# A hybrid attention block on one core: an unused table of taps leaves its buffer to a tile of the compressor's weight

## The chip, the core and the metric

The program runs on one core of a Trainium2 chip. The metric is the device time of one execution in microseconds (us), as the median of several runs. The profile is of one more execution, with its own time. Engines are TensorE (PE; its weight loads are PEld), VectorE (DVE), ScalarE (ACT), GpSimd (POOL) and SyncE (SP, which here only issues loads and stores).

## What is computed

One transformer layer on x of 256 tokens by 1024 features, all in float32: a projection, four mixers side by side (a sparse attention with a compressor, a block attention, a depthwise convolution of 31 taps, a gated recurrence), an output projection, and a feed-forward part of width 4096 between two layer norms.

```python
h = x @ w_in                                   # split by columns into the mixers' inputs
kc = nsa_compress(kc, pe, w1, b1, w2)          # gelu((blocks + pe) @ w1 + b1) @ w2, for k and for v
o_nsa  = nsa_attention(q_n, kc, vc, ks, vs, kw, vw, gates, rel_tab[:4])
o_moba = moba_attention(q_m, k_m, v_m, rel_tab[4:])
o_conv = conformer_conv(conv_in, dw_w, dw_b, cln_g, cln_b, pw_w)
o_hgrn = hgrn2_mixer(q_h, f_h, i_h, g_h, lb, hn_g)
x = layer_norm(ALPHA * x + concat(o_nsa, o_moba, o_conv, o_hgrn) @ w_out, ln1_g, ln1_b)
x = layer_norm(ALPHA * x + square(relu(x @ w_ff1)) @ w_ff2, ln2_g, ln2_b)
```

## The kernel before

**Weights.** Each weight comes in as a raw float32 tile of 128 partitions by 2048 columns, from the pool `raws` (L168), which holds five of them. For most, `Weight.split` (L234) then makes a pair: ACT rounds the raw tile to `hi` (L245), DVE subtracts to get `lo` (L246), and PE multiplies hi by hi, hi by lo and lo by hi. The pools `his` and `los` hold three tiles each. Three chunks (ca, cg, qn) and km are multiplied raw. The projection's weight is cut into chunks by columns, named ca, cg, n1, ni0, ni1, qn, f, q, km, g, qm, vm; "ni0" and "ni1" are two halves of one chunk by rows. In the profile's names the last digits are cut off, so w_n is n1 and w_ni is ni0 or ni1.

**The compressor's weight** w1 comes in four tiles of 1 MB, in two loads of two (`load_w1`, L419: w1a for c = 0, w1b for c = 1). The profile calls them `w<-in_nsa_cmp_w_dram`. `part_cmp` multiplies them in L686, 8 products for each tile, into one bank of PSUM.

**The taps.** L488 and L489 load a table of the convolution's taps, 1 MB, from GpSimd's queue into the tile `tapw`, which has the buffer `mixl` of the pool `wk`. Only the branch `if CONV_T` of `part_conv` would read it, and `CONV_T` is empty. The convolution is done by DVE alone, 62 operations on `yc` (L571, L573). The next tile in that buffer is `mixl`, the low part of the mixers' outputs, written first by the end of the windowed attention.

**Order.** SP issues all loads of weights in the order of the list LOADS as the table below puts them. A load waits for its buffer (the engines that last read it) and for the load that had its semaphore before it: the eight `DMAHW` lanes go round. Each engine works strictly in the order that is written down for it in the table ISSUE (L69), one string of instruction numbers for each engine, so an instruction that waits holds all behind it. The first stage, up to about 112 us, is projections and mixers; then come w_out, the first norm, 16 groups of feed-forward, and the second norm.

**Banks.** The projections' products go to two banks named `mm` (L202), in turn. A chunk's product can begin only when ACT or DVE has copied the bank's content before it: for q and f that is ni's, which ACT copies to `vn` (L645) and `iv` (L345).

Of the kernel before, what the change touches and what calls it, by code (L numbers as in the profile page):

```python
# [9 lines left out]
F32 = mybir.dt.float32  # L10
# [7 lines left out]
P = 128  # L18
S = 256
# [27 lines left out]
def shape_constants():  # L47
# [13 lines left out]
    for i, b in enumerate(LEVELS):  # L61
# [63 lines left out]
    ),  # L125
    Activation=(
# [9 lines left out]
    ),  # L136
    Pool=(
        "20-22 14 23-24 15 2 9-10 13 11-12 0-1 3-8 16-19 25-28 "
    ),
    SP=(  # L140
        "0-10 30 28-29 11-27 31-89 "
# [21 lines left out]
def layer(ctx, tc, I, const, out):  # L163
# [18 lines left out]
    CONV_T = ()  # L182

    LOADS = "ca cg n1 ni0 qn f ni1 qm w1a q km g w1b vm".split()
# [234 lines left out]
    def load_w1(c):  # L419
        res = []  # L420
        at_(R_SPLIT + next(chunk_no))
        for i in range(2):
            raw = raws.tile([P, 2048], F32, name="w1", tag="raw").rearrange("p (a b) -> p a b", a=8)
            nc.sync.dma_start(raw, I["nsa_cmp_w1"][:, c, i])
            res.append(raw)
        return res
# [60 lines left out]

    tapw = wk.tile([P, 8, 8, 32], F32, name="tapw", tag="mixl")  # L488
    late(tapw, I["taps"])  # L489
# [49 lines left out]
    def part_conv():  # L539
        nonlocal pcv, yc  # L540
        at_(K["taps"])
        yc = t2_("c", "yc")
        if CONV_T:

            W, H, n = 28 + S, 31 + S, len(CONV_T)
            hc_d = dr.tile([P, n, H], F32, name="hc_d")
            G.dma_start(hc_d, hc[:, CONV_T[0]:CONV_T[0] + n])
            hcs = wk.tile([P, n, 4, W], F32, name="hcs", tag="hgw")
            for i in range(n):
                for j in range(4):  # L550
                    G.dma_start(hcs[32 * j:32 * j + 32, i],
                                bass.AP(tensor=hc_d.tensor, offset=hc_d.offset + i * H + j,
                                        ap=[[n * H, 32], [32 * n * H, 4], [1, W]]))

            pcv = hbank([P, n, S])
            for i in range(n):
                for b in range(8):
                    for q in range(4):
                        T.matmul(pcv[32 * q:32 * q + 32, i], tapw[:, 4 * CONV_T[i] + q, b], hcs[:, i, q, 4 * b:4 * b + S],
                                 start=(b == 0), stop=(b == 7))  # L560
# [3 lines left out]
        for k in range(31):  # L564
            for i in range(2):
                if i in CONV_T:
                    continue
# [649 lines left out]
```

## Time and profile before

| | us |
|---|---|
| median of 3 runs | 332.45 (331.56 to 332.95) |
| the profiled execution, its own time | 335.78 |
| its span, first to last instruction | 334.0 |
| PE busy in the span | 319.8 (96%) |
| DVE busy | 233.3 (70%) |
| ACT busy | 166.8 (50%) |
| POOL busy | 10.5 (3%) |
| DMA moved | 62.75 MB, mean 188 GB/s |

Busy is the time in which an engine had an instruction running; for PE the ends of products are modelled. "Waits" are idle time of an engine ahead of an instruction, put down to the event that came last. The timeline gives instructions in order of time, equal neighbours merged. Times in it are from the span's start; the profiled execution took 3.33 us more than the median of the runs.

### The profile page before, as it was taken

What the parts mean: (1) busy time and instruction counts of PE and PEld (TensorE: products, weight loads), DVE (VectorE), ACT (ScalarE), POOL (GpSimd) and SP (SyncE); (2) the same over time, 40 slices, a digit from 0 to 9 for tenths busy, and PEclk for the clock granted to TensorE, in tenths of its full rate; (3) what the DMA queues carried; (4) which work ended last, traced back from release to release, by engine and by line L of the source; (5) the groups of instructions that cost most, each with busy time, mean ns of one, the idle gap of its engine ahead of it and who ended that gap; (6) DMA issues with size and microseconds to landing.
All of it is one profiled execution on the core that took longest, in us unless ns stands there. A gap on an engine that the chain in (4) does not pass through costs nothing.

```text
span 334.0 us, 4992 instructions
## 1 busy us (share of the span) xinstructions
PE 319.8 (96%) x1929; PEld 273.1 (82%) x1929; DVE 233.3 (70%) x428; ACT 166.8 (50%) x307; POOL 10.5 (3%) x33
## 2 busy tenths in 40 slices
PE   8999969999999999989999999999999999999990
PEld 6897859898988778788888888888888888888880
DVE  0269969999989866886677477747564756568286
ACT  1464444784899982344365354535453545373100
POOL 3500000000000100000000000100000000000000
PEclk9999998999999999999999999999999999999996
DMA  7999799094300216556567555965565646520012
GB/s 234 387 398 416 235 395 388 15 371 135 121 0 2 54 74 251 153 226 186 214 232 251 176 203 155 318 202 207 153 226 160 219 144 233 156 98 0 2 49 77
DMA packets 18359, 62.75 MB, mean 188 GB/s; under 512 B 1784, under 2 KB 3664, under 8 KB 17696
## 3 DMA queue, kind: packets, MB, share of 16 engines
q1 hardware_dynamic: 15648, 56.61, 47.8%
q0 software_dynamic: 1056, 3.72, 3.2%
q10 hardware_dynamic: 1632, 2.11, 2.2%
q8 instruction: 15, 0.25, 0.3%
q14 instruction: 8, 0.07, 0.1%
HBM read 61.37 MB, written 1.06 MB: 187 GB/s over the span
## 4 chain that ended last, share of the span: by engine, by line
PE 86%; DVE 8%; DMA 2%; ACT 1%; issue 1%; DVEq 0%; ACTq 0%
PE mm L1102 15%; PE mm L1100 8%; PE hg L1121 5%; PE hg L1122 4%; PE tt L1122 4%; PE tt L1120 4%; PE hg L1120 4%; PE tt L1121 4%; DMA w_q_raw<-in_w_in_dram 2%; PE mm_km L310 2%; PE mm L1099 2%; PE mm_cg L310 2%; DVE yc L573 2%; PE acc L292 1%; PE tt L371 1%; PE tt L397 1%
## 5 line engine op out<-in xcount | busy, mean ns | idle before, releaser
L1102 PE MATMUL mm<-x1s,w_hi 128*128 128x512 f32 x210 | 74.4, 394 | 0.0
L246 DVE TENSOR_TENSOR r_lo<-r_raw,r_hi 128x1024 fp32r<-128x1024 f32 x40 | 47.4, 1221 | 24.8 <-ACT r_hi L245 24.8
L1100 PE MATMUL mm<-x1s,w_lo 128*128 128x256 f32 x240 | 61.0, 279 | 0.0
L245 ACT ACTIVATE r_hi<-r_raw 128x1024 fp32r<-128x1024 f32 x40 | 40.6, 1050 | 33.5 <-PE tt L1122 32.4
L1100 PEld LDWEIGHTS mm<-x1s,w_lo 128*128 128x128 f32 x240 | 44.9, 188 | 2.7
L1102 PEld LDWEIGHTS mm<-x1s,w_hi 128*128 128x128 f32 x210 | 39.2, 188 | 7.4
L246 DVE TENSOR_TENSOR w_lo<-w_raw,w_hi 128x1024 fp32r<-128x1024 f32 x32 | 37.8, 1218 | 5.0 <-ACT w_hi L245 5.0
L245 ACT ACTIVATE w_hi<-w_raw 128x1024 fp32r<-128x1024 f32 x32 | 32.2, 1051 | 4.6 <-DMA w_raw<-in_w_ff_dram 4.5
L1106 ACT ACTIVATE fx<-mm 128x256 f32<-128x256 f32 x30 | 11.4, 383 | 44.4 <-PE mm L1102 44.4
L1107 DVE TENSOR_TENSOR fs<-mm,fx 128x256 f32<-128x256 f32 x30 | 12.6, 424 | 28.5 <-ACT fx L1106 28.5
L573 DVE SCALAR_TENSOR_TENSOR yc<-hc,cols,yc 128x256 f32<-128x256 f32 x60 | 27.5, 479 | 0.5
L1121 PE MATMUL hg<-r_lo,fh 128*128 128x512 f32 (+1 forms) x70 | 26.4, 378 | 0.0
L1120 PE MATMUL hg<-r_hi,fh 128*128 128x512 f32 (+1 forms) x70 | 26.4, 377 | 0.0
L1121 PE MATMUL tt<-r_lo,fh 128*128 128x512 f32 x64 | 24.1, 396 | 0.0
L1122 PE MATMUL hg<-r_hi,fl 128*128 128x512 f32 (+1 forms) x70 | 22.4, 376 | 0.0
L1122 PE MATMUL tt<-r_hi,fl 128*128 128x512 f32 x64 | 20.8, 397 | 0.0
L1120 PE MATMUL tt<-r_hi,fh 128*128 128x512 f32 x64 | 20.8, 396 | 0.0
L1121 PEld LDWEIGHTS hg<-r_lo,fh 128*128 128x128 f32 x70 | 13.2, 189 | 2.7
L1122 PEld LDWEIGHTS hg<-r_hi,fl 128*128 128x128 f32 x70 | 13.2, 189 | 2.6
L1120 PEld LDWEIGHTS hg<-r_hi,fh 128*128 128x128 f32 x70 | 13.2, 188 | 2.1
L1121 PEld LDWEIGHTS tt<-r_lo,fh 128*128 128x128 f32 x64 | 12.1, 188 | 2.9
L1122 PEld LDWEIGHTS tt<-r_hi,fl 128*128 128x128 f32 x64 | 12.1, 189 | 2.8
(331 smaller groups left out, 650.7 us busy)
## 6 DMA issues: line engine op xcount, KB each, us to landing
w_raw<-in_w_ff_dram SPq DMA_DIRECT2D x32, 512.0 KB, 4.4
r_raw<-in_w_ff_dram SPq DMA_DIRECT2D x16, 1024.0 KB, 4.9
w<-in_nsa_cmp_w_dram SPq DMA_DIRECT2D x4, 1024.0 KB, 7.6
r_raw<-in_w_out_dram SPq DMA_DIRECT2D x4, 1024.0 KB, 6.1
w_ni_raw<-in_w_in_dram SPq DMA_DIRECT2D x2, 792.0 KB, 11.4
xf<-in_xt_dram ACTq DMA_DIRECT2D x4, 256.0 KB, 6.9
w_ca_raw<-in_w_in_dram SPq DMA_DIRECT2D x4, 256.0 KB, 7.1
w_cg_raw<-in_w_in_dram SPq DMA_DIRECT2D x2, 512.0 KB, 5.8
```

The costliest lines, as they stand in the source:

```text
L245: A.activation(self.h[:, i:j], self.raw[:, i:j], AF.Copy)
L246: self.last = V.tensor_tensor(self.l[:, i:j], self.raw[:, i:j], self.h[:, i:j].bitcast(F32), op=ALU.subtract)
L310: T.matmul(dst[:, i], w.raw[:, k, P * i:P * i + P], xf[:, k], start=(k == 0), stop=(k == KT - 1))
L573: V.scalar_tensor_tensor(yc[:, i], h, w, yc[:, i], op0=ALU.mult, op1=ALU.add)
L1099: T.matmul(flat(pf[i]), h, flat(x1s[:, k]), start=True, stop=False)
L1100: T.matmul(pf[i][:, 0], l, x1h[:, k], start=False, stop=False)
L1102: T.matmul(flat(pf[i]), h, flat(x1s[:, k]), start=False, stop=(k == KT - 1))
L1106: A.activation(lo[:, i], pf[i][:, 1], AF.Copy)
L1107: V.tensor_tensor(sq[:, i], pf[i][:, 0], lo[:, i], op=ALU.add)
L1120: T.matmul(bank_, h, w.h[:, i, sl], start=(g == 0 and i == 0), stop=False)
L1121: T.matmul(bank_, h, w.l[:, i, sl], start=False, stop=False)
L1122: last = T.matmul(bank_, l, w.h[:, i, sl], start=False, stop=(g == NG - 1 and i == 1 and sl.stop != 768))
```

## The change

The table of taps, its tile, its load and the branch that would read it go, on the host too. In `load_w1` the first of the four tiles (c = 0, i = 0) takes the buffer `mixl` in place of one of the five raw ones. In LOADS q moves ahead of w1a. The table ISSUE is new: for PE, DVE and ACT in the first stage, for POOL by one number less, and for SP, where one load (the tile in `mixl`) moves ahead of three small ones. No arithmetic changes.

```diff
@@ ISSUE, one line of PE's and the whole of SP's @@
-        "0-10 12 11 13-14 16 18 15 17 19 21 20 23-35 22 40-41 36 42 37-38 43-45 39 46-81 88-91 82-83 92-95 84-87 "
+        "0-6 8 7 10 9 12 11 13-14 16 15 17 19 18 21 23-33 20 34 22 35 40 36-37 41-46 38 47-59 39 60-79 88-91 80-87 "
...
-        "0-10 30 28-29 11-27 31-89 "
+        "0-10 18 30 28-29 11-17 19-27 31-89 "
@@ layer @@
-    CONV_T = ()
-
-    LOADS = "ca cg n1 ni0 qn f ni1 qm w1a q km g w1b vm".split()
+    LOADS = "ca cg n1 ni0 qn f ni1 qm q w1a km g w1b vm".split()
@@ load_w1 @@
-            raw = raws.tile([P, 2048], F32, name="w1", tag="raw").rearrange("p (a b) -> p a b", a=8)
+
+            pool, tag = (raws, "raw") if c or i else (wk, "mixl")
+            raw = pool.tile([P, 2048], F32, name="w1", tag=tag).rearrange("p (a b) -> p a b", a=8)
             nc.sync.dma_start(raw, I["nsa_cmp_w1"][:, c, i])
@@ layer @@
-    tapw = wk.tile([P, 8, 8, 32], F32, name="tapw", tag="mixl")
-    late(tapw, I["taps"])
@@ part_conv @@
-        if CONV_T:
...
-                if i in CONV_T:
-                    continue
```

In the rows of the order, a name's number is the buffer's, `[waits ...]` lists the engines and lanes whose signal the instruction waits for, and lines of the changed kernel are numbered some 3 to 30 lower. The first place is SP's queue from the load of f to that of q. Before:

```order
L228 DMA w_f_raw_126<-in_w_in_dram 128x1024 [waits DMAHW2_49,PE_49]
L228 DMA w_f_raw_126<-in_w_in_dram 128x1024 [waits DMAHW3_49]
L228 DMA w_ni1_raw_135<-in_w_in_dram 128x1584 [waits DMAHW4_49,PE_49]
L228 DMA w_qm_raw_141<-in_w_in_dram 128x1024 [waits DMAHW5_49,DVE_49]
L228 DMA w_qm_raw_141<-in_w_in_dram 128x1024 [waits DMAHW6_49]
L424 DMA w1_150<-in_nsa_cmp_w1_dram 128x2048 [waits DMAHW7_49,DVE_49]
L424 DMA w1_152<-in_nsa_cmp_w1_dram 128x2048 [waits DMAHW0_49,PE_49]
L228 DMA w_q_raw_154<-in_w_in_dram 128x1024 [waits DMAHW4_49,DMAHW2_49,DVE_49]
L228 DMA w_q_raw_154<-in_w_in_dram 128x1024 [waits DMAHW3_49]
```

and now, from the tile in `mixl` on:

```order
L423 DMA w1_159<-in_nsa_cmp_w1_dram 128x2048 [waits DMAHW7_49]
L904 DMA pw_1269<-in_conv_pw_w_dram 128x2x256 [waits DMAHW0_49]
L664 DMA w2_685<-in_nsa_cmp_w2_dram 128x128 [waits DMAHW1_49]
L666 DMA w2k_687<-in_nsa_cmp_w2_dram 128x256 [waits DMAHW2_49]
L225 DMA w_f_raw_126<-in_w_in_dram 128x1024 [waits DMAHW3_49,DVE_49]
L225 DMA w_f_raw_126<-in_w_in_dram 128x1024 [waits DMAHW4_49]
L225 DMA w_ni1_raw_135<-in_w_in_dram 128x1584 [waits DMAHW5_49,PE_49]
L225 DMA w_qm_raw_141<-in_w_in_dram 128x1024 [waits DMAHW6_49,PE_49]
L225 DMA w_qm_raw_141<-in_w_in_dram 128x1024 [waits DMAHW7_49]
L225 DMA w_q_raw_150<-in_w_in_dram 128x1024 [waits DMAHW0_49,DVE_49]
L225 DMA w_q_raw_150<-in_w_in_dram 128x1024 [waits DMAHW1_49]
L423 DMA w1_161<-in_nsa_cmp_w1_dram 128x2048 [waits DMAHW3_49,PE_49]
```

The load of q has moved ahead of w1a and waits for other lanes and another DVE operation; one w1a tile (w1_159) stands ahead of f, the other (w1_161) behind q.

The second place is ACT around the copy of q's weight, w_q_hi, and the copies that empty ni's two banks, vn and iv (their ends release the banks for the products mm_q and mm_f). Before:

```order
L245 ACTIVATE w_qm_hi_144<-w_qm_raw_141 128x1024 [waits DMAHW5_49,DVE_49,PE_49]
L245 ACTIVATE w_qm_hi_144<-w_qm_raw_141 128x1024 [waits DMAHW6_49]
L245 ACTIVATE w_q_hi_157<-w_q_raw_154 128x1024 [waits DMAHW2_49,DVE_49,PE_49]
L645 ACTIVATE vn_410<-mm_ni0_360 128x140
L645 ACTIVATE vn_410<-mm_ni0_361 128x140
L194 ACTIVATE gate_416<-vn_410 128x24 [waits Activation_49]
L345 ACTIVATE iv_413<-mm_ni0_361 128x256
L345 ACTIVATE iv_413<-mm_ni0_360 128x256
```

and now:

```order
L242 ACTIVATE w_qm_hi_144<-w_qm_raw_141 128x1024 [waits DMAHW6_49,PE_49]
L619 ACTIVATE vn_408<-mm_ni0_359 128x140 [waits PE_49]
L619 ACTIVATE vn_408<-mm_ni0_358 128x140 [waits PE_49]
L242 ACTIVATE w_q_hi_153<-w_q_raw_150 128x1024 [waits DMAHW0_49,DVE_49]
L191 ACTIVATE gate_414<-vn_408 128x24 [waits Activation_49]
L342 ACTIVATE iv_411<-mm_ni0_359 128x256
L192 ACTIVATE gate_414<-gate_414 128x24 [waits Activation_49]
L342 ACTIVATE iv_411<-mm_ni0_358 128x256
L242 ACTIVATE w_q_hi_153<-w_q_raw_150 128x1024 [waits DMAHW1_49]
```

Both copies to vn have moved ahead of w_q_hi, and the second half of w_qm_hi has gone behind iv.

The third place is PE where the products of q end and those of w1b (w1_175, w1_177) begin. Before:

```order
L315 MATMUL mm_q_422<-xs_87,w_q_lo_158 128x256
L313 MATMUL mm_q_422<-xs_87,w_q_hi_157 128x256
L314 MATMUL mm_q_422<-xs_87,w_q_hi_157 128x256
L315 MATMUL mm_q_422<-xs_87,w_q_lo_158 128x256
L686 MATMUL acc_654<-w1_175,blk0_333 32x256 [waits DMAHW1_49]
L686 MATMUL acc_654<-w1_177,blk1_334 32x256 [waits DMAHW2_49]
```

and now:

```order
L312 MATMUL mm_f_534<-xs_87,w_f_lo_130 128x256
L311 MATMUL mm_q_420<-xs_87,w_q_hi_153 128x256
L312 MATMUL mm_q_420<-xs_87,w_q_lo_154 128x256
L660 MATMUL acc_652<-w1_161,blk1_332 32x256
L660 MATMUL acc_652<-w1_159,blk0_331 32x256
L660 MATMUL acc_652<-w1_161,blk1_332 32x256
L660 MATMUL acc_652<-w1_175,blk0_331 32x256 [waits DMAHW1_49]
L660 MATMUL acc_652<-w1_177,blk1_332 32x256 [waits DMAHW2_49]
L660 MATMUL acc_652<-w1_175,blk0_331 32x256
```

Three products of w1a have moved from ahead of mm_q to this place. On SP the loads that feed it were before:

```order
L228 DMA w_g_raw_166<-in_w_in_dram 128x1024 [waits DMAHW7_49,DVE_49]
L228 DMA w_g_raw_166<-in_w_in_dram 128x1024 [waits DMAHW0_49]
L424 DMA w1_175<-in_nsa_cmp_w1_dram 128x2048 [waits DMAHW1_49,PE_49]
L424 DMA w1_177<-in_nsa_cmp_w1_dram 128x2048 [waits DMAHW2_49,PE_49]
L228 DMA w_vm_raw_179<-in_w_in_dram 128x1024 [waits DMAHW3_49,DVE_49,Activation_49]
```

and are now:

```order
L225 DMA w_g_raw_166<-in_w_in_dram 128x1024 [waits DMAHW7_49,DMAHW4_49,DVE_49]
L225 DMA w_g_raw_166<-in_w_in_dram 128x1024 [waits DMAHW0_49]
L423 DMA w1_175<-in_nsa_cmp_w1_dram 128x2048 [waits DMAHW1_49,DVE_49]
L423 DMA w1_177<-in_nsa_cmp_w1_dram 128x2048 [waits DMAHW2_49,DVE_49]
L225 DMA w_vm_raw_179<-in_w_in_dram 128x1024 [waits DMAHW3_49,PE_49]
```

The two tiles of w1b now wait for DVE in place of PE (their buffers were those of qm and q, which DVE's w_qm_lo and w_q_lo read last), and vm, behind them, for PE.

## Rows read from the trace of the kernel before

**Rows 1.** Waits of PE, whole span: waited for, us in total, times, longest.

```profile
PE mm_q L313 <- ACT iv L345: 2.6, 1, 2.6
...
PE mm_ni L335 <- ACT qn L345: 0.7, 1, 0.7
PE mm_ni L336 <- DVE w_ni_lo L246: 0.2, 1, 0.2
```

**Rows 2.** Windows before and after that wait: PE, PEld, DVE, ACT, POOL busy, clock, DMA share, GB/s.

```profile
33.00:43.40 10.40, 9.68 (x52) 8.79 (x52) 10.28 (x19) 4.02 (x4) 0.00 (x0) 1.00 0.83 252
...
48.39:51.75 3.36, 3.36 (x16) 3.36 (x17) 3.33 (x14) 3.10 (x13) 0.00 (x0) 0.51 1.04 423
```

**Rows 3.** Timeline of ACT, 46 to 48.6 us: start, us, what, [idle before <-releaser].

```profile
46.40 1.06 ACT L245 ACTIVATE w_q_hi<-w_q_raw 128x1024 fp32r<-128x1024 f32 x1 [5.42 <-DMA w_q_raw<-in_w_in_dram]
47.37 0.45 ACT L645 ACTIVATE vn<-mm_ni 128x140 f32<-128x140 f32 x2
47.84 0.22 ACT L194 ACTIVATE gate<-vn 128x24 f32<-128x24 f32 x1
47.97 0.64 ACT L345 ACTIVATE iv<-mm_ni 128x256 f32<-128x256 f32 x2
```

**Rows 4.** Timeline of SP's issues, 22 to 47 us; the time spans a group's issues.

```profile
22.89 3.12 SPq L228 DMA_DIRECT2D w_qm_raw<-in_w_in_dram  x2
28.90 4.31 SPq L424 DMA_DIRECT2D w<-in_nsa_cmp_w_dram  x2
39.10 1.07 SPq L228 DMA_DIRECT2D w_q_raw<-in_w_in_dram  x2
...
46.23 0.87 SPq L424 DMA_DIRECT2D w<-in_nsa_cmp_w_dram  x2
```

**Rows 5.** Waits of SP's queue, whole span.

```profile
SPq L228 <- DVE w_ni_lo L246: 5.8, 1, 5.8
```

**Rows 6.** Timeline of PE, 43 to 66 us.

```profile
43.48 1.93 PE L686 MATMUL acc<-w,blk 128*32 128x256 f32 x32
45.34 0.49 PE L371 MATMUL tt<-ksw,qn 64*128 64x128 f32 x4
48.39 0.57 PE L313 MATMUL mm_q<-xs,w_q_hi 128*128 128x256 f32 x1 [2.55 <-ACT iv L345]
...
63.28 1.93 PE L686 MATMUL acc<-w,blk 128*32 128x256 f32 x32
```

**Rows 7.** Timeline of DVE, 27 to 62 us.

```profile
27.08 1.80 DVE L246 TENSOR_TENSOR w_ni_lo<-w_ni_raw,w_ni_hi 128x1584 fp32r<-128x1584 f32 x1
...
47.49 1.23 DVE L246 TENSOR_TENSOR w_q_lo<-w_q_raw,w_q_hi 128x1024 fp32r<-128x1024 f32 x1 [2.93 <-ACT w_q_hi L245]
...
50.91 1.22 DVE L246 TENSOR_TENSOR w_q_lo<-w_q_raw,w_q_hi 128x1024 fp32r<-128x1024 f32 x1
...
57.65 4.40 DVE L573 SCALAR_TENSOR_TENSOR yc<-hc,cols,yc 128x256 f32<-128x256 f32 x9
```

**Rows 8.** DMA issues: out<-in, queue, count, KB each, median us from issue to landing.

```profile
r_raw<-in_w_ff_dram SPq DMA_DIRECT2D x16, 1024.0 KB, 4.9
w<-in_nsa_cmp_w_dram SPq DMA_DIRECT2D x4, 1024.0 KB, 7.6
r_raw<-in_w_out_dram SPq DMA_DIRECT2D x4, 1024.0 KB, 6.1
...
tapw<-in_taps_dram POOLq DMA_DIRECT2D x1, 1024.0 KB, 11.2
```

**Rows 9.** Windows late in the first stage, columns as in rows 2.

```profile
75.00:90.00 15.00, 15.00 (x121) 13.80 (x122) 14.65 (x47) 9.22 (x24) 0.00 (x0) 1.00 0.41 141
...
100.00:112.00 12.00, 12.00 (x128) 9.84 (x121) 11.00 (x35) 11.64 (x32) 0.00 (x0) 1.00 0.01 2
```

**Rows 10.** Window of the first projections, columns as in rows 2.

```profile
5.60:33.00 27.40, 27.24 (x147) 24.00 (x145) 14.97 (x27) 12.26 (x21) 6.02 (x12) 1.00 1.04 401
```

**Rows 11.** Timeline of ACT near 29 us.

```profile
29.43 0.38 ACT L581 ACTIVATE ksw<-mm_n 128x256 f32<-128x256 f32 x1 [4.29 <-PE mm_n L315]
```

More of the change, by code (lines that the diff above doesn't have):

```diff
@@ L111 @@
     DVE=(
[13 rows of a table removed]
[13 rows of a table added]
     ),
     Activation=(
[9 rows of a table removed]
[9 rows of a table added]
     ),
     Pool=(
-        "20-22 14 23-24 15 2 9-10 13 11-12 0-1 3-8 16-19 25-28 "
+        "19-21 13 22-23 14 2 8-9 12 10-11 0-1 3-7 15-18 24-27 "
     ),
     SP=(
-        "0-10 30 28-29 11-27 31-89 "
+        "0-10 18 30 28-29 11-17 19-27 31-89 "
     ),
@@ L539, in part_conv @@
     def part_conv():
-        nonlocal pcv, yc
+        nonlocal yc
         at_(K["taps"])
         yc = t2_("c", "yc")
-        if CONV_T:
[L545 to L560, printed above, removed]
-            for i, c in enumerate(CONV_T):
-                A.activation(yc[:, c], pcv[:, i], AF.Identity, bias=cols[:, R_DB + c:R_DB + c + 1])
         at_(K["tapv"])
@@ L1181, in lay_out @@
                            for r, i, j in CHUNKS.values()], axis=1)
-    dw = a["conv_dw_w"][0]
-    taps = np.zeros((4, 32, 8, 8, 32), np.float32)
-    for k in range(31):
-        for c in range(32):
-            taps[(k + 1) % 4, c, :, (k + 1) // 4, c] = dw[k, c::32]
     brow = np.zeros((40, P), np.float32)
@@ L1192, in lay_out @@
     ff1 = a["w_ff1"][0].reshape(8, P, 16, 256).transpose(1, 2, 0, 3)
-    out = dict(x=a["x"], xt=tiles(a["x"][0].T), w_in=w_in, cols=rows.T, taps=taps.reshape(P, 8, 8, 32), brow=brow,
+    out = dict(x=a["x"], xt=tiles(a["x"][0].T), w_in=w_in, cols=rows.T, brow=brow,
                nsa_cmp_w1=w1, nsa_cmp_w2=w2, rel_bias=a["rel_bias"].T, w_ff1=ff1)
```

91 rows, old and new, of tables (Activation, DVE, PE) are left out of this document.

## Prediction

> **What bounds the kernel now.** I read PE's waits first. PE is busy for 96% of the span, so what can be gained quickly is where it stands still. In the first stage that is one place: mm_q waits 2.6 us; the two waits of mm_ni add 0.7 and 0.2 [rows 1]. The page puts mm_q's wait down to the copies to iv. ACT's timeline shows what was behind that: ACT stood idle for 5.42 us until q's weight had landed, and only then did w_q_hi, and behind it in strict order vn, gate and iv, which empty the two banks that mm_q and mm_f need [rows 3]. So mm_q had lost its weight and its bank to one late load. SP's timeline shows why it was late: q was issued at 39.10, behind the two w1a tiles (28.90 to 33.21) [rows 4], and its queue had waited 5.8 us for DVE's w_ni_lo to free a raw buffer [rows 5].
>
> The wait costs more than itself. PE came back at 48.39 [rows 6], and until 51.75 the granted clock was 0.51, the 1.2 GHz level of 2.4 [rows 2]. After the 0.7 us wait at mm_ni the clock stayed at 1.00 [rows 2]. The second engine to look at is DVE: 14.65 of 15 us are busy late in the stage, where PE has no wait, and ACT is as full in the last 12 us [rows 9].
>
> **The change part by part.** The durations are of the profiled execution, 335.78 us. That is 3.33 above the median of 332.45, so I take differences from there and set them against the median.
>
> *The table, 1 MB.* Its load leaves POOL's queue, and a w1 tile of the same size takes its place among the loads of that time, so the bytes up to about 30 us stay the same. In that stretch DMA is full, 401 GB/s at a share of 1.04 [rows 10]; the table took 11.2 us to land, where 1 MB of w1 took 7.6 [rows 8]. Nobody read it. Its one descriptor issue on POOL has no one behind it who is waited for. Worth nothing by itself; the branch that goes held no instruction.
>
> *q earlier.* One raw buffer is freed for q, since a w1a tile sits in mixl. q now waits for the first w_ni_lo, which ended at 28.88 (27.08 + 1.80) [rows 7] and stands earlier in the new order, and on SP it is behind qm, issued by 26.0 [rows 4]. So q goes out by 28.9 in place of 39.10 and, at the 7.3 us that it needed (46.40 less 39.10), lands by 36.2. It is then needed at 43.5. The late load is gone with 7 us to spare.
>
> *What is late next at mm_q.* ni's last product ended at 43.48, where w1a's products begin [rows 6]. Four small products have moved out from among ni's (0.49 us by the like row), so it ends at 43.0. From there ACT has vn 0.45, w_q_hi 1.06, gate 0.22, iv 0.64 and a second gate 0.22, together 2.6 us [rows 3]: banks free at 45.6, w_q_hi at 44.5. PE meanwhile has w1a, 1.93, less three of its 16 products, 0.36, and twice 0.49 [rows 6]: it arrives at 43.0 + 2.55 = 45.55. The two meet; the wait falls from 2.55 to about 0.05. **Gain 2.5 us.**
>
> *The clock.* 3.36 us at 0.51 would have been 1.71 at full clock. Without the wait there is nothing before it that the trace shows lowering the clock. **Gain 1.65 us.**
>
> *Small waits.* The new order has mm_ni wait for other copies. At best both old waits go (0.9 us); at worst DVE sets the pace. DVE restarts with w_q_lo at 44.5, 3.0 us before 47.49 [rows 7], but half of w_qm_lo (1.22, as w_q_lo) is still to be done. So it is 1.8 us earlier where PE is 4.2 earlier: 2.4 us could come back. I take 0.35, nearer the good end, because the free filler is large: in DVE's queue nine yc operations stand in a row (4.40 us) [rows 7], which no other engine needs before the convolution's end. **Loss 0.35 us, between -0.9 and 2.4.**
>
> *w1b, loads made later.* Its two tiles were issued at 46.23 [rows 4] and now wait for DVE's w_qm_lo and w_q_lo. From w_q_lo's first half to the end of its second, DVE took 4.64 us (47.49 to 52.13) [rows 7]; the new order puts five yc (0.49 each) and half of w_qm_lo (1.22) between: 8.3 us, so the second tile goes out at 44.5 + 8.3 = 52.8. Landing takes 4.9 to 7.6 us for 1 MB [rows 8]: 57.7 to 60.4. I take 5.5, between the two lower rows, as the queue then holds little else: 58.3. PE needs it at 45.6 + 14.9 (48.39 to 63.28 before [rows 6]), less 1.65 of clock, less four transposes that leave (0.49), plus three w1a products (0.36): 58.7. Covered by 0.4 us; the cover before was some 8. vm goes out behind it, when PE has left w1a, some 6 us later than now; its copies on ACT then come at most 1 or 2 us late, and its products are the stage's filler.
>
> *The rest of the new order, POOL's and the tail.* Same instructions, other places; after the first stage PE has no wait by a load. Nothing.
>
> A rule of the Trainium skill speaks against the move of the tile (DMA: Bandwidth & Descriptors, section on queues, rings and completion order): each DMA engine takes turns between queues that have work, while one queue's descriptors begin in order. By it the table on POOL's queue let SP's loads through by turns, and a tile in SP's own queue lets none through. By the bytes alone f lands when it did; by that rule it could land later by the tile's whole time, rival B below.
>
> Sum: 2.5 + 1.65 - 0.35 = 3.8 us; 335.78 becomes 331.98, the median 332.45 becomes **328.65**.
>
> **The rivals.**
>
> *A. DVE sets the pace.* For it: 14.65 of 15 us busy [rows 9], and DVE gets ahead by less than PE. Against: the filler. The loss is 2.4 in place of 0.35: 330.7 us.
>
> *B. f is late.* w1's tile is ahead of f on SP's queue, and the new order has ACT copy f's weight before ksw, which before waited for PE alone, at 29.43 [rows 11]. 1 MB at 401 GB/s [rows 10] is 2.6 us, and a wait of that length has once brought 1.65 us of low clock: 4.25 against a gain of 4.15 (before the small waits), so 332.55. Against: the bytes ahead of f are the same as with the table.
>
> *C. w1b comes late (the slower side).* One mechanism: SP's queue stands until DVE has done w_q_lo, and PE stands at w1b's first products. At 7.6 us a load, landing at 60.4, PE waits 1.7 and loses 1.65 of clock: 332.0. From a landing at 60.85 the gain of 3.8 is eaten (2.15 + 1.65); from 62.5 the kernel is slower by over 0.5%. That needs DVE 2 us later than worked out, say because a reduction that stands ahead of w_q_lo waits for the bias tile. At 63.3: 4.6 + 1.65 - 3.8, so 334.9.
>
> *D. The wait stays in part.* q is there, but w_q_hi, vn and iv still lie between ni's end and mm_q on ACT; if ACT comes 1.5 us late to them, that and the clock remain: 331.8.
>
> **How the numbers follow.** Forecast 0.60, A 0.13, B 0.10, C 0.12, D 0.05. Low end: 332.45 less 4.15 and both small waits, 327.4. High end: 332.2, which takes in A and D and the mild half of C; B's full price and C's bad half, some 0.16, are left out. A measurement can tell about 0.5% (1.66 us) from no change: faster is below 330.8, slower above 334.1. Faster: the forecast, half of A, a little of D: 0.68. Slower: C's bad half and a part of B: 0.10. The rest, 0.22, is no change.
>
> **What would show it.** Right: q issued before 30 us; no wait at mm_q over 0.3 us; granted clock 1.00 from 46 to 60; PE's w1b products at about 59 and everything after it some 4 us earlier. A wait of PE at w1b's first product speaks for C, DVE idle nowhere and several PE waits on DVE between 60 and 112 for A, ACT's w_f_hi idle on DMA for B. A time above 331 makes the prediction wrong.

## The result and the profile after

The changed kernel takes **334.9 us** (median of 6 runs, 334.03 to 335.86), the kernel before 332.54 (6 runs, 331.56 to 332.95). The ratio is 1.0077 with an interval of 1.0055 to 1.0099: slower by 0.8%, where a gain was forecast, 328.65 in a range of 327.4 to 332.2. Of 91 further executions of before one took 338.86 us, the others 331.44 to 333.69.

The profiled execution is one of the six, 334.85 us with a span of 333.1; in it PE is busy for 320.9 us (96%), DVE for 234.2, ACT for 167.3 and POOL for 10.0, and DMA moved 61.70 MB, the 1 MB of the table less.

Yet the profile after shows the steps that the prediction worked out. These are issues of SP's queue:

```profile
18.75 0.81 SPq L225 DMA_DIRECT2D w_f_raw<-in_w_in_dram  x2
...
21.47 3.56 SPq L225 DMA_DIRECT2D w_qm_raw<-in_w_in_dram  x2
25.51 0.80 SPq L225 DMA_DIRECT2D w_q_raw<-in_w_in_dram  x2
...
49.60 2.28 SPq L423 DMA_DIRECT2D w<-in_nsa_cmp_w_dram  x2
```

q goes out at 25.51 in place of 39.10 [rows 4]. PE's waits have no mm_q left, and none at w1b:

```profile
PE acc L1025 <- DVE scale L1018: 1.5, 1, 1.5
PE acc L289 <- DVE idle L286: 1.2, 1, 1.2
PE mm_ni L332 <- DVE blk L569: 0.6, 1, 0.6
PE hg L1025 <- DVE scale L1018: 0.5, 1, 0.5
```

mm_q begins at 44.91 in place of 48.39 [rows 6], at full clock, and w_out's first product at 108.03 in place of 111.78, which is 3.75 us earlier. So the front did what it was worked out to do, against the execution that was profiled. The kernel is slower all the same, and the first thing to look at is therefore what that execution was. Before was profiled a second time, unchanged; that execution took 332.46 us, its span is 330.7, and its PE waits read:

```profile
PE hg L1051 <- DVE scale L1044: 1.3, 1, 1.3
PE acc L292 <- DVE idle L289: 1.2, 1, 1.2
PE mm_ni L335 <- ACT qn L345: 0.7, 1, 0.7
PE mm_ni L336 <- DVE w_ni_lo L246: 0.2, 1, 0.2
```

The wait of 2.6 us at mm_q [rows 1], on which the prediction rests, is not in it, nor in the profiles of the three kernels below that change before only elsewhere. It was not typical. Against this typical execution the change stands as follows; the times are starts on PE, in us from the start of the span:

| | before, again | after | after later by |
|---|---|---|---|
| mm_q | 46.52 | 44.91 | -1.61 |
| first product of w_out | 108.38 | 108.03 | -0.35 |
| last product of w_out | 136.22 | 136.44 | 0.22 |
| first product of ff1 | 142.87 | 145.19 | 2.32 |
| last product | 322.12 | 324.51 | 2.39 |

PE's lead at mm_q is mostly work put off to later: from there to w_out PE has no wait in either, and it takes 1.26 us longer. Most of the loss of 2.39 us arises in one place, between the last product of w_out and ff1: the first norm. Its rows of PE in the change (L1022 adds the bias, bsum; L1025 transposes and scales, "hg" and "acc" being the two halves of the columns; the first scale is that of rows 0 to 127, the second that of rows 128 to 255):

```profile
136.75 0.70 PE L1022 MATMUL acc<-bhot,bsum 40*128 40x512 f32 x2
138.00 1.16 PE L1025 MATMUL hg<-scale,x 128*128 128x128 f32 x8 [0.54 <-DVE scale L1018]
139.08 0.48 PE L1022 MATMUL hg<-bhot,bsum 40*128 40x512 f32 x1
141.11 2.07 PE L1025 MATMUL acc<-scale,x 128*128 128x128 f32 x8 [1.54 <-DVE scale L1018]
142.97 1.53 PE L1025 MATMUL hg<-scale,x 128*128 128x128 f32 x8
144.34 1.06 PE L1025 MATMUL acc<-scale,x 128*128 128x128 f32 x8
145.19 0.39 PE L1063 MATMUL mm<-x1s,w_hi 128*128 128x256 f32 x1
```

and in the second profile of before:

```profile
136.53 0.70 PE L1048 MATMUL acc<-bhot,bsum 40*128 40x512 f32 x2
137.07 0.59 PE L1048 MATMUL hg<-bhot,bsum 40*128 40x512 f32 x2
137.70 1.16 PE L1051 MATMUL acc<-scale,x 128*128 128x128 f32 x8
138.70 1.06 PE L1051 MATMUL hg<-scale,x 128*128 128x128 f32 x8
141.02 1.16 PE L1051 MATMUL hg<-scale,x 128*128 128x128 f32 x8 [1.26 <-DVE scale L1044]
142.02 1.06 PE L1051 MATMUL acc<-scale,x 128*128 128x128 f32 x8
142.87 0.38 PE L1089 MATMUL mm<-x1s,w_hi 128*128 128x256 f32 x1
```

Three things are new: a wait of 0.54 us for the first scale; three groups of transposes behind the second scale in place of two; and the first of them takes 141.11 to 142.97, 1.86 us where it takes 1.0 (141.02 to 142.02) before. The windows of 141 to 145 us (PE, PEld, DVE, ACT, POOL busy, clock, DMA share, GB/s) say why, the first line from the change, the second from before:

```profile
141.00:145.00 4.00, 3.89 (x22) 3.89 (x23) 1.98 (x4) 0.96 (x2) 0.00 (x0) 0.63 0.62 249
```

```profile
141.00:145.00 4.00, 3.98 (x33) 3.98 (x34) 3.18 (x5) 2.14 (x3) 0.00 (x0) 1.00 0.56 222
```

The granted clock is 0.63 there on average and 0.50 from 141.0 to 143.5, so a good part of these transposes ran at 1.2 GHz.

### The profile page after: what moved, and what is told of

The parts are those of the page before. It is cut to its first block, busy times and chain, and to the rows that moved or that the text cites. A ratio compares the mean times of both kernels' runs of the same rounds, so it can differ in the third digit from the quotient of the medians.

```text
span 333.1 us, 4995 instructions
## 1 busy us (share of the span) xinstructions
PE 320.9 (96%) x1929; PEld 272.9 (82%) x1929; DVE 234.2 (70%) x428; ACT 167.3 (50%) x307; POOL 10.0 (3%) x32
## 2 busy tenths in 40 slices
DMA packets 18215, 61.70 MB, mean 185 GB/s; under 512 B 1768, under 2 KB 3648, under 8 KB 17680
## 4 chain that ended last, share of the span: by engine, by line
PE 90%; DVE 4%; DMA 3%; issue 1%; ACT 1%; ACTq 0%; DVEq 0%
PE mm L1076 15%; PE mm L1074 8%; PE hg L1095 5%; PE hg L1096 5%; PE hg L1094 4%; PE tt L1096 4%; PE tt L1094 4%; PE tt L1095 4%; DMA w_f_raw<-in_w_in_dram 3%; PE mm L1073 2%; PE mm_km L307 2%; PE mm_cg L307 2%; PE tt L368 2%; PE acc L289 1%; PE tt L394 1%; PE acc L660 1%
## 5 line engine op out<-in xcount | busy, mean ns | idle before, releaser
L374 ACT ACTIVATE p<-p,mx 128x256 f32<-128x256 f32 (+1 forms) x24 | 10.7, 446 | 7.7 <-DVE mx L371 7.7
```

The costliest lines, as they stand in the source:

```text
L374: A.activation(pr_[:, h], pr_[:, h], AF.Exp, scale=-1.0, bias=mx[:, h:h + 1], accum_out=sm[:, h:h + 1])
```

## The experiments

Two theories were set against each other. **Theory 1:** the profiled execution of before was untypical, the front's gain is not there at the median, and the loss is the new order behind the front. **Theory 2:** the wait at mm_q is there in every execution, and the front loses elsewhere what it wins. (Each ratio is to executions of before that ran beside: 332.26 us over 29 of them, 332.01 over 11, 332.31 over 21 or 332.29 over 18.)

### Is the gain there?

**Before, unchanged.**

> The kernel before, unchanged, to see a typical execution of it. Theory 1 (the profiled execution, 335.8 us, was untypical: its wait at mm_q and the low clock behind it are mostly absent at the median): spans about 330.8, and a profile near the median shows mm_q waiting 1 us or less. Theory 2 (the wait of 2.55 us is there in every execution and the time is made up elsewhere): mm_q waits 2.3 to 2.7 us in a profile near 332.5 us too.

332.36 us over 12 runs, 331.55 to 333.34; none comes near the 335.78 of the profile that the prediction read. The waits stand above. What differed shows in ACT's timeline of this execution:

```profile
39.72 2.01 ACT L245 ACTIVATE w_qm_hi<-w_qm_raw 128x1024 fp32r<-128x1024 f32 x2 [3.91 <-PE mm_ni L337]
44.34 1.06 ACT L245 ACTIVATE w_q_hi<-w_q_raw 128x1024 fp32r<-128x1024 f32 x1 [2.61 <-PE mm_ni L337]
```

w_q_hi runs at 44.34, and what ended ACT's idle time was PE and no longer the landing of q. q was issued no earlier, at 39.85 against 39.10 [rows 4], but its transfer took 4.7 us in place of 7.6 (the medians of issue to landing of its two halves):

```profile
w_q_raw<-in_w_in_dram SPq DMA_DIRECT2D x2, 512.0 KB, 4.7
```

So q was late because its transfer was slow, and it was not the only one: the 1 MB load of toep on ACT's queue, in flight with it, took 8.8 us in place of 5.9, and from 37 to 40 us DMA moved 138 GB/s in place of 284. Theory 1 holds, as far as the gain goes. Why transfers were slow in that one execution stays open.

**The change's loads with the old order.** The tile in mixl, q ahead of w1a, no taps; the tables of PE, DVE and ACT are those of before.

```diff
     ISSUE: PE, DVE, Activation as in the kernel before
     ISSUE: Pool, SP as in the change
```

> The change's tile and loads (no taps, one w1 tile in mixl, q ahead of w1a) with the order of PE, DVE and ACT of before. Theory 1: the late q cost little at the median, so 332.0 to 332.8. Theory 2: mm_q's wait was always there and goes now, 328.5 to 330.5.

332.53 us, ratio 1.0009 (0.9995 to 1.0022): the loads alone are worth nothing. q went out ten microseconds earlier:

```profile
29.73 0.80 SPq L227 DMA_DIRECT2D w_q_raw<-in_w_in_dram  x2
```

and nobody was waiting for it. Theory 2's 328.5 to 330.5 falls.

**A q that is made late.** The table of taps is loaded twice more between w1a and q.

```diff
     late(tapw, I["taps"])
+    for i in range(2):
+        nc.sync.dma_start(tapw, I["taps"])
```

> Before, with the table of taps loaded twice more (2 MB) on SP's queue between w1a and q: in typical executions of before q lands just in time, so this makes it late by up to 5 us. The prediction's price (2.55 us of wait cost 4.2 with the low clock behind it) says 335 to 338 us; PE waits 2 to 4 us at mm_q, clock near 0.5 behind it. If the wait costs only itself: 334 to 336, clock 1.00 throughout.

339.2 us over 4 runs, ratio 1.0219 (1.0196 to 1.0242), more than expected, as mm_q waits longer than expected. In the profile (its span is 339.0, its own time of 340.81 lies 1.6 above the median of its runs) mm_q waits 6.10 us:

```profile
52.50 0.58 PE L314 MATMUL mm_q<-xs,w_q_hi 128*128 128x256 f32 x1 [6.10 <-ACT iv L346]
```

```profile
52.50:54.50 2.00, 2.00 (x9) 2.00 (x10) 1.97 (x12) 2.00 (x7) 0.00 (x0) 0.50 1.02 412
54.50:56.50 2.00, 2.00 (x11) 2.00 (x10) 2.00 (x5) 1.09 (x7) 0.00 (x0) 0.50 1.04 420
56.50:58.50 2.00, 2.00 (x15) 1.90 (x14) 1.96 (x7) 0.00 (x0) 0.00 (x0) 0.85 1.03 422
58.50:62.00 3.50, 3.50 (x29) 3.08 (x29) 2.32 (x11) 1.08 (x4) 0.00 (x0) 1.00 0.99 404
```

These windows lie behind it: 4 us at 0.50 and 2 at 0.85 lose 2.0 + 0.3 = 2.3 us of clock. Wait and clock make 8.4 us, and this span is 8.3 longer than that of the second profile of before (339.0 less 330.7). So the prediction's way to price such a wait, itself and the low clock behind it, is right. The wait was not there to be removed.

**The wait that is left in before.** The copy to qn moves ahead of the second half of w_f_hi on ACT.

```diff
-    Activation: ... 31 12-13 37 32 14 ...
+    Activation: ... 31 12 37 13 32 14 ...
```

> Before, with ACT's copy to qn moved ahead of the second half of w_f_hi: it removes the only PE wait of a typical execution in the front that is over 0.5 us (0.69 us at mm_ni). Theory 1 (PE's waits are all there is to gain in the front): 0.4 to 0.7 us faster, 331.4 to 331.8 where before is 332.1. Theory 2 (the next copy or the next weight takes its place): within 0.2 us of before.

332.15 us, 0.9994 (0.9981 to 1.0007), and the wait of 0.69 us is still there: the copy now waits for PE's own last product of mm_qn, so the wait is the copy itself. Theory 2 holds here. A typical execution of before has no wait in the front that an earlier copy or load would take away.

### Where does the loss come from?

**The norm's order alone, both ways.** In the change, the norm's instructions of all three engines go back into the order of before; and the other way round in before. The numbers 719 to 726 are the transposes of rows 0 to 127, 729 to 736 those of rows 128 to 255.

```diff
-    PE: ... 718 728 719-722 727 733-736 729-732 723-726 737-749 ...
+    PE: ... 718 728 727 723-726 719-722 729-749 ...
```

> The change, with the first norm's instructions on PE, DVE and ACT put back into the relative order of before. Theory 1 (the change's front is worth about 0.3 us at the median, and its order of the first norm costs 2.1 to 2.5 us): 332.5 us, against 332.5 of before no difference, ff1 begins 6.4 us after the last product of w_out. Theory 2 (the loss lies elsewhere, the norm's order is worth 0.3 us at most): 334.6 us or more.

334.63 us, 1.0072 (1.0053 to 1.0091): not to be told from the change. The norm itself is shorter (7.0 us from the first bsum at 137.43 to ff1 at 144.44, where the change takes 8.4), but in this execution the first bsum came 0.7 us later than in the change's (136.75), and 0.57 us were lost at once at the feed-forward's first weight, which ACT now splits too late:

```profile
146.82 0.50 PE L1074 MATMUL mm<-x1s,w_hi 128*128 128x512 f32 x1 [0.57 <-ACT w_hi L243]
```

> Before, with the change's relative order in the first norm alone. Theory 1: 2 us slower, 334.6 us, ff1 begins 8.5 us after the last product of w_out. Theory 2: within 0.3 us of before, 332.5.

333.82 us, 1.0049 (1.0028 to 1.0069). Theory 1 got the size and the place wrong. Three groups of transposes behind the second scale took 140.66 to 143.40, 2.74 us at full clock, so this norm is only 0.2 us longer than before's; 0.80 us of the rest is again a wait at the feed-forward's weight:

```profile
148.89 0.50 PE L1101 MATMUL mm<-x1s,w_lo 128*128 128x256 f32 x2 [0.80 <-DVE w_lo L247]
```

So the three groups by themselves cost little at full clock, and a piece of one order set into another makes waits of its own. Two of the 12 executions, 335.53 and 335.86 us, list a mean clock of 0.986 where the other ten list 0.991 to 0.995; no trace shows where it fell in them.

**All that lies behind w_out.** First norm, feed-forward and second norm of the change in the order of before; and the other way round, there with w_out itself too.

```diff
     (in the change)
-    PE, DVE, Activation: behind w_out as the change has them
+    PE, DVE, Activation: behind w_out in the relative order of before
```

> The change, with all instructions behind w_out (first norm, feed-forward, second norm) on PE, DVE and ACT back in the relative order of before; the front and w_out stay the change's. Theory 1 (the change's front is worth nothing against a typical execution, as PE does not wait there; the loss of 2.2 us is the order behind w_out, and what the norm's order alone gave back was lost again at the first feed-forward product): 332.2 to 332.9 us, no PE wait over 1.4 us behind w_out, 185.9 us from the last w_out product to the last product. Theory 2 (the loss is the front's, which leaves other engines late): 334 us or more.

333.87 us, 1.0051 (1.0038 to 1.0065): some 0.9 us of the loss go, not 2.2, so the time of neither theory is met exactly. PE now waits twice in the norm, at full clock:

```profile
139.16 1.16 PE L1026 MATMUL acc<-scale,x 128*128 128x128 f32 x8 [0.94 <-DVE scale L1019]
140.15 1.06 PE L1026 MATMUL hg<-scale,x 128*128 128x128 f32 x8
142.47 1.16 PE L1026 MATMUL hg<-scale,x 128*128 128x128 f32 x8 [1.26 <-DVE scale L1019]
```

> Before, with all instructions of w_out and behind it in the change's relative order; its loads and its front stay. Theory 1: about 2.2 us slower, 334.2 to 335.0, with 188.0 us from the last w_out product to the last product. Theory 2: 332.3 to 332.9.

336.99 us, 1.0141 (1.0122 to 1.016), twice what was expected. The change's norm came back as it was, with waits of 0.55 and 1.55 us and the clock at 0.58 in the 4 us behind them; w_out, torn out of its front, waited for r_lo and mixl as well (0.6 and 0.4). It shows the norm's loss as a thing that goes with the order of w_out, and its size proves nothing.

**One subtraction.** In the change the second half's subtraction of rows 0 to 127 (228) goes ahead on DVE, and its transposes ahead of the second wait on PE.

```diff
-    PE: ... 719-722 727 733-736 729-732 723-726 737-749 ...
+    PE: ... 719-726 727 733-736 729-732 737-749 ...
-    DVE: ... 226 231-232 ... 238 237 228 240 242 ...
+    DVE: ... 226 228 231-232 ... 238 237 240 242 ...
```

> The change, with two things moved in the first norm: the second half's subtraction of rows 0 to 127 goes ahead of the second 128 rows' work on DVE, and its 8 transposes ahead of the wait for the second scale on PE. Theory 1: one of three groups of transposes leaves the stretch behind the wait (1.05 us, and some 1 us of low clock less), DVE is 0.7 us later: 333.0 to 333.9. Theory 2: 334.6 to 335.2.

334.49 us, 1.0072 (1.0056 to 1.0087), so no measurable gain. In the profiled execution the clock stayed at 1.00, but DVE was later: the waits for the two scales are 1.2 and 0.7 us, 1.9 where the change has 2.1, and a third of 0.7 came at ff1. (The other five executions list a mean clock of 0.990 to 0.991 where this one has 0.995, so theirs may have fallen.)

**The clock alone.** First the change itself once more.

> The change itself, beside the next kernels: 334.4 to 335.2 us, and again a wait of about 1.5 us for the second scale in the first norm, with low clock on the transposes behind it. If the low clock there was an accident of one execution, the transposes advance at 0.125 us each and the first norm takes 7.4 us in place of 8.75.

335.08 us, 1.0084 (1.0069 to 1.0099); waits of 0.54 and 1.55, and the clock from 141 to 145 is 0.57. It is no accident of one execution: of the ten timed executions of the change nine list a mean clock of 0.988 to 0.990 over the span, and the one with 0.993 is the fastest, 334.03 us. Then the change with 7 products that nobody reads put into the two waits:

```diff
+            if t == 0:
+                spare = [mmbank()[:, 0, :P] for _ in range(2)][0]
+                for _ in range(7):
+                    T.matmul(spare, ident, ident, start=True, stop=True)
```

> The change, with 7 products that nobody reads (identity by identity, into a bank that is free) in PE's two waits of the first norm: 2 ahead of the first transposes, 5 ahead of the transposes behind the second scale. The waits themselves stay. Theory 1 (about 1.3 us of the loss is low clock that the two waits bring): clock 1.00 from 136 to 150, 8 transposes in 1.0 us, 333.1 to 333.9 us. Theory 2 (the loss is the waits and the third group of transposes alone): 334.6 to 335.2.

334.03 us, 1.0051 (1.0039 to 1.0064), 1.05 us faster than the change beside it and just above the range of theory 1; its five executions list a mean clock of 0.992 to 0.995:

```profile
138.08 0.71 PE L1026 MATMUL mm<-cc 128*128 128x128 f32 x4
138.69 1.16 PE L1031 MATMUL hg<-scale,x 128*128 128x128 f32 x8
139.78 0.48 PE L1028 MATMUL hg<-bhot,bsum 40*128 40x512 f32 x1
140.19 1.38 PE L1026 MATMUL mm<-cc 128*128 128x128 f32 x10
141.80 1.16 PE L1031 MATMUL acc<-scale,x 128*128 128x128 f32 x8 [0.23 <-DVE scale L1020]
142.80 1.06 PE L1031 MATMUL hg<-scale,x 128*128 128x128 f32 x8
```

The second scale comes no earlier (the transposes behind it begin at 141.80, in the run beside it at 141.76), but each group of transposes takes 1.0 us again. This part of the loss is TensorE's clock, and work without use gives it back.

**The front alone.** In the change the last part of w_out, too, goes back into the order of before.

```diff
     (in the change)
+    PE: products 669 and above but 717 in the relative order of before
+    DVE from 218, Activation from 166: in the relative order of before
```

> The change, with the last part of w_out (all of rows 128 to 255 and the second half of rows 0 to 127) and everything behind it back in the relative order of before; the front alone stays the change's. Theory 1 (the 0.7 us that the run with the tail alone left in the norm comes from w_out's order, which finishes rows 0 to 127 later): 6.6 to 6.8 us from the last w_out product to ff1, no wait for the first scale, 332.6 to 333.4 us. Theory 2 (the front leaves DVE and ACT late, and w_out's order only follows from that): the wait of 0.9 us stays, 333.7 or more.

333.38 us, 1.0028 (1.0017 to 1.0038). The wait for the first scale fell from 0.94 to 0.26 and the norm has the length of before (6.64 us from the last product of w_out to ff1, in before 6.65); theory 1 holds, though at the upper edge. 1.07 us remain, and they lie ahead of w_out's last part. Two runs asked where.

```diff
-    PE: 717 among the products of w_out
+    PE: ... 718 728 717 727 ...
```

> The version with the change's front alone (w_out's last part and all behind it in the order of before), with the one bsum product that the change does among the products of w_out put back behind them. Theory 1 (it costs 0.4 us there and saves nothing behind, where PE only waits longer for the first scale): 0.3 to 0.4 us faster than that version, +0.7 us against before, w_out's stage 28.0 us long in place of 28.5, no wait for the first scale. Theory 2 (it is neutral, 0.3 us come back as a fourth bsum product in the norm): +0.9 to 1.2 us.

333.48 us, 1.0034 (1.0022 to 1.0045): neutral, theory 2. The last one also moves ACT's three copies to ksw ahead of the first half of w_f_hi:

```diff
-    Activation: ... 29 12 34-36 32 13 37 ...
+    Activation: ... 29 34-36 12 32 13 37 ...
```

> The same version, and ACT's three copies to ksw ahead of the first half of w_f_hi, as before had it, so that they no longer wait for f's landing. Theory 1 (what is left of the front's loss is PE's wait at mm_ni, 0.6 to 1.5 us in the change's profiles, and it comes from f): no wait over 0.3 us at mm_ni, 332.0 to 332.7 us, within 0.2 per cent of before. Theory 2 (f's wait was covered by the later start of other work; the loss is spread over the front's products): +0.7 us as the version without it.

332.48 us, 1.0011 (0.9999 to 1.0024): 1.0 us faster than the version beside it (0.7 by the means), and not to be told from before. The first fence is ACT without that last edit, the second with it:

```profile
27.99 1.06 ACT L243 ACTIVATE w_f_hi<-w_f_raw 128x1024 fp32r<-128x1024 f32 x1 [4.06 <-DMA w_f_raw<-in_w_in_dram]
...
28.95 0.37 ACT L556 ACTIVATE ksw<-mm_n 128x256 f32<-128x256 f32 x1
```

```profile
27.60 0.39 ACT L556 ACTIVATE ksw<-mm_n 128x256 f32<-128x256 f32 x1 [3.46 <-PE mm_n L313]
...
28.79 2.01 ACT L243 ACTIVATE w_f_hi<-w_f_raw 128x1024 fp32r<-128x1024 f32 x2
```

With the edit ksw waits for PE alone, and PE's wait at mm_ni (1.6 us in the profile without it) is gone. That wait is put down to DVE's blk, and blk without the edit stood behind ksw:

```profile
30.19 1.24 DVE L570 TENSOR_TENSOR blk<-mm_n,cols 64x240 f32<-64x240 f32 x3 [1.55 <-ACT ksw L559]
```

Set one after the other, the medians account for the loss: from 335.08 for the change, 1.05 us go with the clock (334.03); 0.65 with the rest of the order behind the front (333.38); 1.0 with f's landing ahead of ksw (333.48 to 332.48). By the means the three are 1.1, 0.7 and 0.7 us, so each is known to some tenths only. What is left is not to be told from before. No version came out measurably faster than before.

## Why the prediction was wrong, point by point

**The step that failed first** is the sentence that the profiled execution stands 3.33 us above the median, "so I take differences from there and set them against the median". That takes the difference for something that both kernels have. It was the very wait that the change was to remove: 2.55 of wait and 1.65 of clock, 4.2 us in all, less 0.8 by which that execution came earlier to mm_ni (33.53 against 34.30 in the second profile), are 3.4 us, and the two spans differ by 3.3 (334.0 and 330.7). A typical execution had paid none of it. The gain of 4.15 us was right for the execution that was read, and zero for the median.

**q earlier, the wait, the clock.** As mechanisms right: q went out at 25.51 (forecast: by 28.9), mm_q did not wait, the clock was 1.00. The run with a late q shows that the price was right too (8.4 us worked out that way, 8.3 in the span). Their value at the median is 0.

**The table and its load.** Worth nothing, as said: the change's loads with the old order measured 1.0009.

**w1b and vm.** w1b's two tiles went out between 49.60 and 51.88, the forecast had 52.8 for the second; PE did not wait for them in this profile, and 0.3 us at most in the others. Rival C, the only one on the slower side, did not come about; that the time fell at the upper end of its prices is chance.

**Small waits.** The term of 0.35 us was mis-sized. A wait at mm_ni stayed, 0.6 to 1.6 us in all but one of the profiles with ACT's new order, and its mechanism is the second half of rival B: ACT takes f's weight ahead of ksw, and ksw's bank is what mm_ni needs. It cost 0.7 to 1.0 us, where B had 0.10 of chance and a price of 4.25. f itself took 9.0 to 9.5 us from issue to landing in the ten profiles with the tile on SP's queue, and 8.0 to 8.7 in the five typical ones with the table on POOL's (10.0 in the one that was read). By the rule of the Trainium skill that stood beside B (DMA: Bandwidth & Descriptors, queues, rings and completion order) the tile ahead of f could make f later. The traces agree in the direction, by 0.3 to 1.5 us counted from the issue, and not with the tile's whole time, 2.6 us; counted from the span's start f's first half lands at 27.2 to 29.1 with the tile and at 27.2 to 28.1 without. No run took the tile out of SP's queue with the new order kept, so what part this had in the wait stays open.

**"The rest of the new order ... Nothing"** is the second step that failed. The reason given, same instructions in other places, and no PE wait by a load behind the first stage, looks at loads only. Nor is the order new in the first stage alone, as is said ahead of the prediction: of PE's 787 places that hold another instruction, 148 lie behind w_out, 13 of them in the first norm. The waits in the norm are for DVE's two scales, and the one for the second stands in before's own page of waits too, with 1.3 us. The new order has w_out finish rows 0 to 127 later and puts more transposes behind the second scale. That cost 0.65 us, and 1.05 us of clock on top of it, by the medians. The places of the order that the prediction compared were those around the loads; the norm's 20 PE instructions were not among them.

**The bound by DVE** (rival A) did not decide: behind mm_q PE has no wait up to w_out.

## What to carry to other kernels

When the execution that was profiled is slower than every timed run, ask first whether the wait you mean to remove is what made it so: compare the wait and what it costs with the difference, and if they are alike, expect no gain at the median until a second profile shows the wait again. Where a change brings a new order, go through each place in which an engine already waits, also far behind the edit, and compare what stands on either side of the wait. A short wait at a place full of small products can cost a good part of its length again in clock (here 1.05 us with waits of 0.54 and 1.54), and a few products that nobody reads, set into it, are a cheap way to find out how much.

## What the runs showed of the hardware

TensorE's granted clock fell within a wait of 1.54 us (139.57 to 141.11 in the change's profile) that had a wait of 0.54 us and 1.6 us of work ahead of it: it was 1.00 up to 140.5, 0.54 in the half microsecond behind that, 0.50 from 141.0 to 143.5 and 1.00 again from 144.0. It did not fall after waits of 0.94 and 1.26 us that lay 2.05 us of transposes apart (the run with the order behind w_out put back), nor after the single 1.26 of before. Waits of like sum, 2.1 and 2.2 us, thus went with low clock in one place and with none in the other; what decides was not tried apart. And q's load, two halves of 0.5 MB issued at the same place of the program, took 4.7 us in one execution and 7.6 in another (the median of the halves), which made a wait that with its low clock moved the end by some 3 us.
